# The order of the combined blocks in a two-layer trunk: T1, T2, T3, T4 for all features

## The chip, the cores and the metric

One core of a Trainium2 chip. The time is that of one execution on the device, in microseconds (us); the time of a kernel is the median of its runs.

## The reference

A trunk of two layers over 1024 positions of 1024 features. A mixer (gated delta rule in layer 0, retention in layer 1) and a feed-forward part with a causal convolution, each with a modulation before it and a layer norm behind it:

```python
D_MODEL = 1024; SEQ = 1024; DEPTH = 2; FFN_HIDDEN = 2816; FFN_CONV = 3
def conv_ffn(h, w_up, conv_w, conv_b, w_down):
    gate, up = jnp.split(h @ w_up, 2, axis=-1)
    gate = causal_dwconv(gate, conv_w) + conv_b
    return (jax.nn.silu(gate) * up) @ w_down
...
    for i in range(DEPTH):
        ...
        y = mixers[i % N_MIXERS](x * (1.0 + sc1) + sh1)
        x = layer_norm(DN_ALPHA * x + (1.0 + g1) * y, ln_g[i, 0], ln_b[i, 0])
        y = conv_ffn(x * (1.0 + sc2) + sh2, ffn_up[i], ffn_conv_w[i], ffn_conv_b[i], ffn_down[i])
        x = layer_norm(DN_ALPHA * x + (1.0 + g2) * y, ln_g[i, 1], ln_b[i, 1])
```

All of it is float32. The part that matters here is `h @ w_up` of both layers and retention's `h @ w_in`: a matrix of 1024 x 1024 activations times wide weights.

## The kernel before

Engines: PE does the matmuls, DVE (VectorE) tensor operations, ACT (ScalarE) activations and copies, SP issues most DMAs. Each engine works through its own queue in order; the order of each queue is set by the scheduler of the language's tile layer, which places instructions as their inputs are expected, so a change in the program text moves rows on every engine.

**A float32 matmul in three.** An operand is split into a rounded high part and the rest: ACT copies (`split`, L89), DVE subtracts (L90). `mm3` (L108 on) then does three matmuls, low x high, high x low and high x high, which appear as L110, L111 and L112 (or L1159, where a product is added to an accumulator that already holds one). A block of weights split in this way is called wb (512 wide) or wh and wl (1024 wide).

**Seven products in place of eight.** `strassen` multiplies 2 x 2 blocks of the activations (11, 12, 21, 22, by halves of features and of positions) with 2 x 2 blocks of the weights by the Strassen-Winograd scheme. It runs three times: for the input of the FFN of layer 0 (about 745 to 1190 us in the profile), for the input of retention (1425 to 1690) and for the FFN of layer 1 (2255 to 2700). The first two weight pairs are done plainly (`side`), while the activation blocks are still being made. From the third pair on, `wino` makes the seven products in this order: 11; 21; s1 with T1; s2 with T2 (added to the first); s4 with 22; s3 with T3; the last with T4. s1 to s4 are sums of weight blocks (`psub`, L1205), made by DVE into one of two `mm` PSUM banks and then split.

**The combined blocks.** T1 = 12 - 11, T3 = 22 - 12, T2 = T3 + 11, T4 = 21 - T2, each in four features k. `build_T` makes 12 and 22 (transposed on PE, scaled by ACT at L403 into a buffer bt, split), and returns `rest()`, which makes T1 to T4. `rest()` is called after the first weight pair's second half has been emitted. Blocks 11 and 21 exist only in split form; `joined` (L409) adds the two parts again by two matmuls with an identity into one of the two `mm` banks, which the transposes and the psubs use as well. Before, one join of 11 per feature served T2 and T1, and one join of 21 served T4. The rows of DVE are L423 (T3), L425 (T2), L427 (T1) and L429 (T4).

**Buffers.** `tags` names the pool of each block, in the order T1, T2, T3, T4, 22. A plain block 12 uses the pool of T1, so T1 can be split only when the last product on that block 12 is done.

Beside this, DVE does the convolution of the gate (L1584 three-operand rows, L1598 additions, L1570), the modulation of the next stage (L221, L223) and the weight splits. Line numbers above are those before; behind the change lines from L429 on stand one further down (L1205 is L1206, L1584 is L1585, L1159 is L1160).

Of the kernel before, what the change touches and what calls it, by code (L numbers as in the profile page):

```python
# [24 lines left out]
NF = F // P  # L25
# [8 lines left out]
def trunk_kernel(ctx: ExitStack, tc, A):  # L34
    nc = tc.nc
    pe, act, dve, pool, sp = nc.tensor, nc.scalar, nc.vector, nc.gpsimd, nc.sync
# [12 lines left out]
    def two(tag, dt=F32, name=None):  # L49
        if tag in ("qkv", "auh"):  # L50
            return tl(tag, [P, HALF], dt, name), tl(tag, [P, HALF], dt, name)
        t = tl(tag, [P, 2, HALF], dt, name)
        return t[:, 0], t[:, 1]
# [332 lines left out]

    def build_T(B, xts, scale, shift, tags):
        tags = dict(zip(("T1", "T2", "T3", "T4", "22"), tags))
        tags["12"] = tags["T1"]
        for nm in tags:  # L390
            B[nm] = [None] * 4

        def put(nm, k, src, eng=dve):
            t = two(tags[nm], F32R, nm)
            split(t[0], t[1], src, eng)
            B[nm][k] = t

        def load(f, tag):
            pt = mm_tile()
            for t in range(4):  # L400
                pe.transpose(pt[:, t * P:(t + 1) * P], xts[t][:, f * P:(f + 1) * P], ident)
            tmp = tl(tag, [P, HALF], name="bt")
            act.activation(tmp, pt, AF.Identity, bias=shift[:, f:f + 1], scale=scale[:, f:f + 1])  # L403
            return tmp

        def joined(hl):
            pt = mm_tile()
            for n, t in enumerate(hl):
                pe.matmul(pt, ident_r, t, start=n == 0, stop=n == 1)  # L409
            return pt  # L410

        raw = []
        for k, tg in enumerate((("qkv", "qkv"), ("qkv", "qkv"), ("t2", "t2"), ("t2", "ada"))):
            b12, b22 = load(k, tg[0]), load(4 + k, tg[1])
            put("12", k, b12)
            put("22", k, b22)
            raw.append((b12, b22))

        def rest():
            for k in range(4):  # L420
                t1, b22 = raw[k]
                x11 = joined(B["11"][k])
                dve.tensor_sub(b22, b22, t1)  # L423
                put("T3", k, b22)
                dve.tensor_add(b22, b22, x11)  # L425
                put("T2", k, b22)
                dve.tensor_sub(t1, t1, x11)  # L427
                put("T1", k, t1)
                dve.tensor_sub(b22, joined(B["21"][k]), b22)  # L429
                put("T4", k, b22)  # L430

        return rest
# [663 lines left out]
    for nm in ("S", "T0", "Dt", "M", "Tq"):  # L1096
# [4 lines left out]
    items = [("h", 1), ("h", 2), ("h", 3), (c, K + 3), (c, V), (c, V + 1), (c, 0), (c, 1), (c, V + 2), (c, V + 3), (c, 2), (c, 3),  # L1101
             (c, K + 4), (c, K + 5), (c, K + 6), (c, K + 7), (c, V + 4), (c, V + 5), (c, 4), (c, 5), (c, V + 6), (c, V + 7), (c, 6), (c, 7)]
# [47 lines left out]
        dve.tensor_tensor(b, a, b, ALU.add)  # L1150
        return b

    def strassen(hT0, xts, scale, shift, items, tags=("hTb", "hTb", "qkv", "qkv", "aux"), direct=False, beside=None, spare="lane"):
        B = {"11": hT0[:4], "21": hT0[4:]}
        nblk = [0]
        nacc = [0]

        def mm_on(*a, **kw):
            return pe.matmul(*a, skip_group_check=True, **kw)  # L1159

        def side(n, s):
            out = []
            for u in items[n][:2]:
                w = load_w(u)
                X = acc_tile()
                for i, b in enumerate((("11", "21"), ("12", "22"))[s]):
                    for k in range(4):
                        mm3(X, w, k + 4 * i, B[b][k], i == 0 and k == 0, i == 1 and k == 3)
                out.append(X)
            return out  # L1170

        ahead, sinks = [], []
        for n in range(2):
            X = side(n, 0)
            if direct:
                sinks.append(items[n][2]())
                for i in range(2):
                    sinks[n](2 * i, X[i], None)
                continue
            ahead.append([tl("cv", [P, 516], name="ah")[:, 0:HALF] for _ in range(2)])  # L1180
            for t, x in zip(ahead[n], X):
                act.activation(t, x, AF.Copy)
        rest = build_T(B, xts, scale, shift, tags)

        def block(src):
            n = nblk[0]
            nblk[0] += 1
            t = tl(("wh", "wl")[n % 2], [P, 2, HALF], F32R, name="wb")
            split(t[:, 0], t[:, 1], src)
            return kn(t[:, 0]), kn(t[:, 1])  # L1190

        def prod(src, b, onto=None):
            w = block(src)
            if onto is None:
                nacc[0] += 1
                acc = (acc_tile, acc_tile, sc_tile)[nacc[0] % 3]()
            else:
                acc = onto
            for k in range(4):
                mm3(acc, w, k, B[b][k], onto is None and k == 0, k == 3, mm_on if onto is not None else pe.matmul)  # L1200
            return acc

        def psub(x, y, op=ALU.subtract):
            t = mm_tile()
            dve.tensor_tensor(t, x, y, op)  # L1205
            return t  # L1206

        def wino(n, sink):
            ua, ub = items[n][:2]
            raws = []  # L1210
            for m, u in ((2 * n, ua), (2 * n + 1, ub)):
                if direct and m % 3 == 0:
                    raws += [tl("xT", [P, HALF], name="wr") for _ in range(2)]
                    for h2 in range(2):
                        anchor["i"] = sp.dma_start(raws[-2 + h2], u[:, hs(h2)])
                else:
                    w = tl("wr", [P, D])
                    anchor["i"] = sp.dma_start(w, u)
                    raws += [w[:, hs(0)], w[:, hs(1)]]
            if beside:  # L1220
                beside(n)
            a11, a12, a21, a22 = raws
            def copy_of(X, tag="cv"):
                t = tl(tag, [P, 516] if tag == "cv" else [P, HALF], name="pc")[:, 0:HALF]
                act.activation(t, X, AF.Copy)  # L1225
                return t

            X = prod(a11, "11")
            p1 = copy_of(X)
            s1 = psub(a21, a22, ALU.add)  # L1230
            sink(0, prod(a12, "21"), p1)
            s2 = psub(s1, a11)
            Z = prod(s1, "T1")
            z5 = copy_of(Z)
            s4 = psub(a12, s2)
            prod(s2, "T2", X)
            u2 = copy_of(X)
            s3 = psub(a11, a21)
            prod(s4, "22", Z)
            sink(1, Z, u2)  # L1240
            bg_step()
            prod(s3, "T3", X)
            u3 = copy_of(X, "t2")
            sink(3, X, z5)
            sink(2, prod(a22, "T4"), u3)
            bg_step()

        bg_tag[0] = spare
        for n in range(2):
            if not direct:  # L1250
                sinks.append(items[n][2]())
                for i in range(2):
                    sinks[n](2 * i, ahead[n][i], None)
            X = side(n, 1)
            for i in range(2):
                sinks[n](2 * i + 1, X[i], None)
            if n == 0:
                rest()
            if items[n][3]:
                items[n][3]()  # L1260
        for n in range(2, len(items)):
            wino(n, items[n][2]())
            if items[n][3]:
                items[n][3]()
        bg_tag[0] = "wr"
        return B
# [267 lines left out]
    def layer_tail(i, mix, wout, xsrc, x_mid, x_out, ln_next, final):  # L1534
        sc2, sh2 = fold(i, 1, 2 * i)
        if i == 0:
            hT0 = []
            get = out_hl(mix)
            G1 = rows[0, 2]
            xts = proj_ln(0, GH, get, wout, xsrc, G1, ("x", i))  # L1540
            hooks = ln_hooks(0, xts, "hTa", lambda: (sc2, sh2), hT0, x_mid, ("mid", i), BAL["gh"])
            xts = proj_ln(1, GH, get, wout, xsrc, G1, ("x", i), hooks=hooks, tag="aux")
# [3 lines left out]
        else:  # L1546
            mix.append((sc2, sh2))
            hT0, xts = proj_st(mix[0])
# [8 lines left out]
        spare = ("aux", "lane")[i]  # L1557
# [50 lines left out]

            return [(up[4 * fp], up[4 * fp + 2], gate_start, conv), (up[4 * fp + 1], up[4 * fp + 3], up_start, None)]

        strassen(hT0, xts, sc2, sh2, [it for fp in range(NF // 2) for it in pair_items(fp)], ("hTb", "hTb", "qkv", "qkv", ("lane", "aux")[i]), spare=spare)
        slots = {"c": "hTa", "x": "qkv"}
        gb2 = gain_rows(3, ("mid", i), "hTb") if final else None
        return proj_st(proj_gen(NF // 2, ablk_of(ad, "qkv"), A["ffn_down"][i], slots, xg[i + 1], rows[i, 5],
# [21 lines left out]
    h0, xts = layer_tail(0, raws, A["gdn_wout"], xin, xs[0], xs[1], next0, False)  # L1636
# [54 lines left out]
    sc_r, sh_r = next0()  # L1691
# [18 lines left out]
    order = units[:2]  # L1710
    for n in range(6):
        order += ropes[n + (n + 1) // 3:n + 1 + (n + 2) // 3] + [units[2 + n]]
    B = strassen(h0, xts, sc_r, sh_r, order, ("hTa", "aux", "qkv", "qkv", "hTa"), True, scale_rows)
    hT = [h0, []]
    xlo = []
    for t in range(4):
# [276 lines left out]
```

## Time and profile before

| | us |
|---|---|
| median of 3 runs | 2937.2 (2934.97, 2937.2, 2941.72) |
| profiled execution | 2931.49 |
| its span | 2929.3 |
| PE busy in it | 2808.1 |
| DVE busy in it | 2198.4 |
| granted TensorE clock, mean | 0.989 |

A row of a timeline has the start, the length, engine, line, operation and the tiles (written <- read); in brackets what the engine waited for just before it. A row of a window has the busy time and the number of instructions of PE, weight load, DVE, ACT and POOL, then the granted clock of PE (1.00 is full speed), the share of the DMA engines and GB/s. A matmul of a timeline row is shown with its whole length; the next one starts before it ends, so the starts count.

### The profile page before, as it was taken

How to read it: one execution, taken by the hardware profiler on the slowest of the kernel's cores; microseconds unless marked ns; L12 is line 12 of the kernel's file. 1: busy time of each engine (PE TensorE's matmuls, PEld its weight loads, DVE VectorE, ACT ScalarE, POOL GpSimd, SP SyncE). 2: the span in 40 equal slices, each digit the busy share in tenths (PEclk: the TensorE clock that was granted, in tenths of full speed). 3: DMA queues.
4: the chain of work that ended last, by engine and by line, in shares of the span. 5: the costliest groups of instructions: out<-in, count | busy, mean ns of one | idle time of the engine just before them, and what ended most of it. 6: DMA issues, size and time to landing. Idle time of an engine off the chain costs nothing. (4 is left out here: it accounts for less than half of the span.)

```text
span 2929.3 us, 38823 instructions
## 1 busy us (share of the span) xinstructions
PE 2808.1 (96%) x13638; PEld 2296.3 (78%) x13638; DVE 2198.4 (75%) x3965; ACT 1316.2 (45%) x2457; POOL 421.1 (14%) x485
## 2 busy tenths in 40 slices
PE   8998999999999999999999999999999899999997
PEld 7777877887778888887787877777778688888786
DVE  6695687556788888897687766666697887778888
ACT  3755465443544444536443332221345544444443
POOL 0311220134011111100000000223201011111001
PEclk9999999999999999999999999999999999999999
DMA  8122221354344444863434454555564233335753
GB/s 309 64 80 80 98 91 44 105 187 148 108 150 159 163 157 147 316 218 123 157 110 173 149 181 149 165 172 163 189 235 155 94 137 108 108 108 202 262 158 119
DMA packets 239234, 442.35 MB, mean 151 GB/s; under 512 B 22848, under 2 KB 76352, under 8 KB 239040
## 3 DMA queue, kind: packets, MB, share of 16 engines
q1 hardware_dynamic: 206832, 387.96, 39.4%
q10 hardware_dynamic: 29760, 43.00, 4.0%
q0 software_dynamic: 2448, 8.91, 0.8%
q8 instruction: 107, 1.75, 0.2%
q14 instruction: 87, 0.71, 0.1%
HBM read 331.26 MB, written 108.53 MB: 150 GB/s over the span
## 5 line engine op out<-in xcount | busy, mean ns | idle before, releaser
L1466 PE MATMUL acc<-bb,ab 128*128 128x512 f32 x1800 | 427.5, 393 | 6.5 <-DVE pa L1441 2.5
L1466 PEld LDWEIGHTS acc<-bb,ab 128*128 128x128 f32 x1800 | 338.0, 189 | 81.4 <-DVE bb L90 3.8
L630 PE MATMUL acc<-hT,wh 128*128 128x512 f32 x960 | 300.3, 394 | 0.0
L1605 POOL TENSOR_TENSOR o<-o 128x512 f32<-128x512 f32 x88 | 121.1, 1387 | 810.6 <-DVE o L1598 680.4
L89 ACT ACTIVATE ab<-ar 128x512 fp32r<-128x512 f32 x210 | 129.0, 624 | 184.2 <-PE acc L1466 93.3
L1159 PE MATMUL acc<-T,wb 128*128 128x512 f32 x840 | 204.2, 392 | 7.2 <-DVE wb L90 7.2
L630 PEld LDWEIGHTS acc<-hT,wh 128*128 128x128 f32 x960 | 183.0, 191 | 34.0
L630 PE MATMUL acc<-hT,wl 128*128 128x512 f32 x480 | 202.8, 422 | 0.8 <-DVE qkv L993 0.5
L1159 PEld LDWEIGHTS acc<-T,wb 128*128 128x128 f32 x840 | 157.9, 189 | 43.7 <-DVE wb L90 11.1
L90 DVE TENSOR_TENSOR ab<-ar,ab 128x512 fp32r<-128x512 f32 x210 | 146.4, 703 | 44.2 <-ACT ab L89 44.2
L90 DVE TENSOR_TENSOR wb<-mm,wb 128x512 fp32r<-128x512 f32 x216 | 145.2, 684 | 23.4 <-ACT wb L89 21.7
L90 DVE TENSOR_TENSOR wb<-wr,wb 128x512 fp32r<-128x512 f32 x162 | 111.3, 688 | 65.7 <-ACT wb L89 63.8
L1225 ACT ACTIVATE pc<-acc 128x512 f32<-128x512 f32 x143 | 84.7, 592 | 160.5 <-PE acc L1159 91.6
L89 ACT ACTIVATE wh<-wr 128x1024 fp32r<-128x1024 f32 x101 | 107.0, 1061 | 110.2 <-PE acc L630 50.3
L89 ACT ACTIVATE wb<-mm 128x512 fp32r<-128x512 f32 x216 | 122.3, 593 | 72.8 <-DVE mm L1205 72.1
L90 DVE TENSOR_TENSOR wl<-wr,wh 128x1024 fp32r<-128x1024 f32 x85 | 105.5, 1241 | 61.2 <-ACT wh L89 59.1
L89 ACT ACTIVATE wb<-wr 128x512 fp32r<-128x512 f32 x162 | 99.7, 627 | 96.5 <-DMA wr<-in_ffn_up 53.0
L449 DVE SCALAR_TENSOR_TENSOR qkv<-raw,vc,qkv 128x512 f32<-128x512 f32 x144 | 112.3, 783 | 34.8 <-ACT qkv L447 30.7
L630 PE MATMUL acc<-wh,hT 128*128 128x512 f32 x384 | 135.5, 415 | 0.7 <-DVE vv L90 0.7
L1584 DVE SCALAR_TENSOR_TENSOR o<-g,vc,o 128x512 f32<-128x512 f32 (+2 forms) x176 | 135.2, 786 | 0.7
L223 DVE SCALAR_TENSOR_TENSOR ada<-mvw,e,ada 128x512 f32<-128x512 f32 x140 | 105.9, 757 | 27.0 <-DMA mvw<-in_ada_w 26.5
L110 PE MATMUL acc<-T,wb 128*128 128x512 f32 x292 | 116.6, 399 | 9.9 <-DVE wb L90 9.4
(626 smaller groups left out, 6876.5 us busy)
## 6 DMA issues: line engine op xcount, KB each, us to landing
wr<-in_ffn_up SPq DMA_DIRECT2D x96, 512.0 KB, 4.3
ad<-o SPq DMA_DIRECT2D x154, 256.0 KB, 2.2
ar<-ad SPq DMA_DIRECT2D x154, 256.0 KB, 4.2
mvw<-in_ada_w SPq DMA_DIRECT2D x48, 512.0 KB, 5.5
Br<-in_ffn_down SPq DMA_DIRECT2D x66, 256.0 KB, 3.3
mvw<-in_ada_w SPq DMA_DIRECT2D x64, 256.0 KB, 3.0
wr<-in_ret_wv SPq DMA_DIRECT2D x32, 512.0 KB, 4.2
ar<-od SPq DMA_DIRECT2D x56, 256.0 KB, 5.0
```

The source lines that it names most:

```text
L89: act.activation(dst_h, src, AF.Copy)
L90: eng.tensor_tensor(dst_l, src, dst_h, ALU.subtract)
L110: mm(acc, wl[:, k], hl[0], start=first, stop=False)
L223: dve.scalar_tensor_tensor(a, wr[kk], e[:, k:k + 1], a, ALU.mult, ALU.add)
L449: dve.scalar_tensor_tensor(oh, raw[:, 3 - j:515 - j], w[:, 3 - j:4 - j], oh, ALU.mult, ALU.add)
L630: pq(pe.matmul(out, lhsT, rhs, start=start, stop=stop, **kw), cost)
L1159: return pe.matmul(*a, skip_group_check=True, **kw)
L1225: act.activation(t, X, AF.Copy)
L1466: mm_ = (lambda *a, p=p, onto=onto, **kw: (mm if p < 2 else pe.matmul)(*a, skip_group_check=onto, **kw))
L1584: dve.scalar_tensor_tensor(tv, gv[:, c0 - j:c1 - j], w[:, 2 - j:3 - j], tv, ALU.mult, ALU.add)
L1605: pool.tensor_tensor(o[d], o[x], o[y], op)
```

## The change

`rest()` makes T1 for all four features, then T2, then T3, then T4. T2 is now 22 - T1, without a join; T3 is T2 less a second join of 11, written into the buffer of T1's sum. The pools of T1 and T4 are exchanged in the FFNs (T1 now in `qkv`, T2 and T4 in `hTb`) and in retention (T1 in `qkv`, T4 in `hTa`), and block 12 shares the pool of T4.

```diff
-        tags["12"] = tags["T1"]
+        tags["12"] = tags["T4"]
...
         def rest():
-            for k in range(4):
-                t1, b22 = raw[k]
-                x11 = joined(B["11"][k])
+            for k, (t1, b22) in enumerate(raw):
+                dve.tensor_sub(t1, t1, joined(B["11"][k]))
+                put("T1", k, t1)
+            for k, (t1, b22) in enumerate(raw):
                 dve.tensor_sub(b22, b22, t1)
-                put("T3", k, b22)
-                dve.tensor_add(b22, b22, x11)
                 put("T2", k, b22)
-                dve.tensor_sub(t1, t1, x11)
-                put("T1", k, t1)
+            for k, (t1, b22) in enumerate(raw):
+                dve.tensor_sub(t1, b22, joined(B["11"][k]))
+                put("T3", k, t1)
+            for k, (t1, b22) in enumerate(raw):
                 dve.tensor_sub(b22, joined(B["21"][k]), b22)
                 put("T4", k, b22)
...
-    def strassen(hT0, xts, scale, shift, items, tags=("hTb", "hTb", "qkv", "qkv", "aux"), direct=False, beside=None, spare="lane"):
+    def strassen(hT0, xts, scale, shift, items, tags=("qkv", "hTb", "qkv", "hTb", "aux"), direct=False, beside=None, spare="lane"):
...
-        strassen(hT0, xts, sc2, sh2, [it for fp in range(NF // 2) for it in pair_items(fp)], ("hTb", "hTb", "qkv", "qkv", ("lane", "aux")[i]), spare=spare)
+        strassen(hT0, xts, sc2, sh2, [it for fp in range(NF // 2) for it in pair_items(fp)], ("qkv", "hTb", "qkv", "hTb", ("lane", "aux")[i]), spare=spare)
...
-    B = strassen(h0, xts, sc_r, sh_r, order, ("hTa", "aux", "qkv", "qkv", "hTa"), True, scale_rows)
+    B = strassen(h0, xts, sc_r, sh_r, order, ("qkv", "aux", "qkv", "hTa", "hTa"), True, scale_rows)
```

The number of operations stays the same on DVE and ACT; PE gets four more joins in each of the three stages. The queues differ as follows.

DVE in FFN 0 before, from the last T4 subtraction (the buffer bt_7129 is that of the last feature) to the split of s1 (mm_7422 holds s1, and wb_7443 is its split, for which T1's product waits). s1 itself was formed three rows above this piece:

```order
L429 TENSOR_TENSOR bt_7129<-mm_7293,bt_7129 128x512
L1205 TENSOR_TENSOR mm_7441<-mm_7422,wr_7400 128x512
L90 TENSOR_TENSOR T4_7298<-bt_7129,T4_7297 128x512
L1584 SCALAR_TENSOR_TENSOR o_7301<-g_7137,vc_153,o_7301 128x511
L1570 TENSOR_TENSOR g_7398<-sc_7427,pc_7420 128x512
L1584 SCALAR_TENSOR_TENSOR o_7306<-g_7137,vc_153,o_7306 128x512
L1584 SCALAR_TENSOR_TENSOR o_7301<-g_7137,vc_153,o_7301 128x510
L1584 SCALAR_TENSOR_TENSOR o_7311<-g_7138,vc_153,o_7311 128x511
L1584 SCALAR_TENSOR_TENSOR o_7316<-g_7138,vc_153,o_7316 128x512
L1584 SCALAR_TENSOR_TENSOR o_7306<-g_7137,vc_153,o_7306 128x512
L90 TENSOR_TENSOR wb_7443<-mm_7422,wb_7443 128x512
```

Behind the split of s1 stand, before, two more rows of this convolution and its four L1598 rows, two rows of the next convolution, two of the modulation and the third psub, and then the split of s2.

The same place after the change, from just behind the last T4 subtraction to the splits of s1 (mm_7434, wb_7455) and s2 (mm_7453, wb_7475):

```order
L1599 TENSOR_TENSOR o_7328<-o_7328,acc_7374 128x512
L1206 TENSOR_TENSOR mm_7434<-wr_7414 128x512
L90 TENSOR_TENSOR T4_7303<-bt_7109,T4_7303 128x512
L1585 SCALAR_TENSOR_TENSOR o_7554<-g_7410,vc_153,o_7554 128x511
L90 TENSOR_TENSOR T4_7310<-bt_7129,T4_7310 128x512
L1206 TENSOR_TENSOR mm_7453<-mm_7434,wr_7412 128x512
L1585 SCALAR_TENSOR_TENSOR o_7554<-g_7410,vc_153,o_7554 128x510
L221 TENSOR_SCALAR ada_7510<-mvw_7511,e_162 128x512
L90 TENSOR_TENSOR wb_7455<-mm_7434,wb_7455 128x512
L223 SCALAR_TENSOR_TENSOR ada_7510<-mvw_7511,e_162,ada_7510 128x512
L1206 TENSOR_TENSOR mm_7473<-wr_7412,mm_7453 128x512
L90 TENSOR_TENSOR wb_7475<-mm_7453,wb_7475 128x512
```

s1 is now formed behind all the T4 subtractions but ahead of two of their splits, and all eight L1585 rows and four L1599 rows of the earlier tile stand above the split of s1. Between the second feature's T1 subtraction and that split there are 51 rows.

PE in retention before, from the last products on block 11 (hT) to T1:

```order
L110 MATMUL sc_13233<-hT_12317,wb_13230 128x512
L111 MATMUL sc_13233<-hT_12317,wb_13230 128x512
L112 MATMUL sc_13233<-hT_12317,wb_13230 128x512
L110 MATMUL acc_13252<-T1_13055,wb_13249 128x512
L111 MATMUL acc_13252<-T1_13055,wb_13249 128x512
```

And after:

```order
L112 MATMUL sc_13257<-hT_12319,wb_13254 128x512
L409 MATMUL mm_13155<-hT_12329,ident_r_727 128x512 x2
L110 MATMUL sc_13257<-hT_12329,wb_13254 128x512
L111 MATMUL sc_13257<-hT_12329,wb_13254 128x512
L112 MATMUL sc_13257<-hT_12329,wb_13254 128x512
L110 MATMUL acc_13276<-T1_13058,wb_13273 128x512
L111 MATMUL acc_13276<-T1_13059,wb_13273 128x512
```

The last join of block 21 (mm_13155) has come to stand three matmuls ahead of T1's product; in FFN 0 it stands directly ahead of it.

DVE in retention after the change, behind that join:

```order
L430 TENSOR_TENSOR bt_12978<-mm_13155,bt_12978 128x512
L1151 TENSOR_TENSOR pc_13250<-sc_13257,pc_13250 128x512
L1206 TENSOR_TENSOR mm_13271<-mm_13252,wr_13230 128x512
L90 TENSOR_TENSOR T4_13159<-bt_12978,T4_13159 128x512
L90 TENSOR_TENSOR wb_13273<-mm_13252,wb_13273 128x512
```

The split of s1 (wb_13273), for which T1's product waits, stands four rows behind the last T4 subtraction. Before, it stood three rows behind it, and that subtraction's join stood 25 matmuls ahead of T1.

## The prediction

> **What bounds the kernel now.** I read the page's head first, then its costliest groups, then the list of PE's waits around the two feed-forward (FFN) stages where the combined blocks are made, and last the timelines of PE and DVE there.
>
> ```profile
> span 2929.3 us, 38823 instructions
> PE 2808.1 (96%) x13638; PEld 2296.3 (78%) x13638; DVE 2198.4 (75%) x3965; ACT 1316.2 (45%) x2457; POOL 421.1 (14%) x485
> ...
> L1159 PE MATMUL acc<-T,wb 128*128 128x512 f32 x840 | 204.2, 392 | 7.2 <-DVE wb L90 7.2
> ```
>
> PE is busy for 96% of the span, so only two things move the end: matmuls added or removed, and stretches in which PE stands or runs slowly. The last row is the products on combined blocks: they wait for DVE's split of a weight block (wb, L90). PE's waits in FFN 0 and, below the dots, FFN 1 (us in total, times, longest):
>
> ```profile
> PE acc L110 <- DVE wb L90: 4.7, 1, 4.7
> PE acc L1159 <- DVE wb L90: 1.9, 1, 1.9
> PE mm L409 <- DVE bt L429: 0.3, 1, 0.3
> ...
> PE acc L1159 <- DVE wb L90: 1.8, 1, 1.8
> PE sc L1159 <- DVE wb L90: 0.8, 1, 0.8
> ```
>
> FFN 1 has the 4.7 us too. PE's timeline says where (start, length; the wait in brackets): FFN 0, then FFN 1.
>
> ```profile
> 800.26 0.39 PE L112 MATMUL sc<-hT,wb 128*128 128x512 f32 x1
> 805.34 0.79 PE L110 MATMUL acc<-T,wb 128*128 128x512 f32 x1 [4.69 <-DVE wb L90]
> 805.93 0.63 PE L111 MATMUL acc<-T,wb 128*128 128x512 f32 x1
> 810.20 0.55 PE L112 MATMUL acc<-T,wb 128*128 128x512 f32 x1
> 812.64 4.41 PE L1159 MATMUL acc<-T,wb 128*128 128x512 f32 x12 [1.89 <-DVE wb L90]
> 819.84 0.39 PE L110 MATMUL acc<-T,wb 128*128 128x512 f32 x1
> ...
> 2313.50 0.79 PE L110 MATMUL acc<-T,wb 128*128 128x512 f32 x1 [4.69 <-DVE wb L90]
> 2323.64 0.84 PE L1159 MATMUL acc<-22_20065,wb 128*128 128x512 f32 x3
> 2326.36 0.39 PE L110 MATMUL acc<-T,wb 128*128 128x512 f32 x1
> ```
>
> The row at 805.34 is the first product on T1, 812.64 that on T2, then come the 12 matmuls on block 22, and 819.84 is the first on T4. FFN 1 is the same 1508.16 us later (2313.50 - 805.34), but its T4 starts at 2326.36, which is 818.20 on FFN 0's scale. At full speed a matmul is issued every (2326.36 - 2323.64)/12 = 0.227 us; T1 after its wait ran at (810.20 - 805.93)/10 = 0.427 us. The clock granted in these stretches (PEclk is the third number from the end):
>
> ```profile
> 805.30:810.75 5.45, 5.41 (x12) 3.79 (x12) 5.45 (x10) 2.55 (x5) 0.00 (x0) 0.52 0.13 50
> 815.00:817.00 2.00, 2.00 (x6) 1.52 (x6) 1.28 (x2) 0.60 (x1) 1.92 (x3) 0.50 0.14 25
> 2321.00:2325.00 4.00, 4.00 (x18) 3.28 (x18) 3.34 (x4) 1.09 (x2) 3.84 (x4) 1.00 0.44 150
> ```
>
> So the 4.69 us wait costs more than itself: T1's 12 matmuls took 5.41 us where 12 x 0.227 = 2.72 would do, a loss of 2.69. In FFN 0 the next 24 (812.64 to 819.84, 7.20 us against 5.44) lost 1.76 more. DVE's timeline shows why PE waited:
>
> ```profile
> 789.02 1.29 DVE L90 TENSOR_TENSOR wb<-wr,wb 128x512 fp32r<-128x512 f32 x2 [2.02 <-ACT wb L89]
> 796.16 1.29 DVE L90 TENSOR_TENSOR T<-bt,T 128x512 fp32r<-128x512 f32 x2
> 797.36 0.68 DVE L429 TENSOR_TENSOR bt<-mm,bt 128x512 f32<-128x512 f32 x1
> 801.29 3.39 DVE L1584 SCALAR_TENSOR_TENSOR o<-g,vc,o 128x512 f32<-128x512 f32 x5
> 804.60 0.69 DVE L90 TENSOR_TENSOR wb<-mm,wb 128x512 fp32r<-128x512 f32 x1
> 811.90 1.28 DVE L90 TENSOR_TENSOR wb<-mm,wb 128x512 fp32r<-128x512 f32 x2
> ```
>
> The split at 804.60 (s1) frees T1, the one at 811.90 (s2) frees T2. DVE is an in-order queue that works through without a gap there, and what counts is how many rows stand ahead of these two. Two rows of one tensor operation take (797.36 - 796.16) = 1.20, so 0.60 each; the convolution's rows (L1584) take 3.39/5, so 0.66 at their spacing.
>
> **The change, part by part.**
>
> *Operations.* DVE and ACT do the same number of them: per feature four subtractions and four splits stay. PE gets one more join of block 11 per feature, 4 in each of three stages (two FFNs and retention's input). What a join costs:
>
> ```profile
> 772.52 1.20 PE L409 MATMUL mm<-hT,ident_r 128*128 128x512 f32 x4 [0.58 <-ACT bt L403]
> ...
> 791.55 0.62 PE L409 MATMUL mm<-hT,ident_r 128*128 128x512 f32 x2
> 792.01 0.40 PE L111 MATMUL acc<-22_7074,wh 128*128 128x512 f32 x1
> ```
>
> 792.01 - 791.55 = 0.46, so 1.84 per stage and 5.5 in all. In the FFNs PE waits for DVE behind them, so the joins lie inside that wait and I charge nothing more; without that wait they would cost the full 3.7. In retention part of it is on the path, below.
>
> *FFN 0.* In the changed DVE queue the four T4 subtractions and splits, and the convolution's eight L1585 and four L1599 rows, all stand ahead of the split of s1. I walk the queue. T1 of the second feature needs its join, which before was one of the two at 772.52 and now stands behind 24 matmuls more (5.4 us, less the 1.0 of the wait and the join that no longer stand there): it runs from 776.95 to 777.4, and DVE starts that subtraction at about 777.65. From there to the end of the split of s1 stand 51 rows: 38 of 0.60, 2 splits of a 128x1024 block at 1.14, 10 three-operand rows at 0.66 and one of 0.4. That is 22.9 + 2.3 + 6.6 + 0.4 = 32.2, so 809.9, and T1 starts at 810.0 in place of 805.34. The PE queue is done with the products before it at about 801.8, so the wait grows from 4.69 to about 8.2. But the split of s2 now stands only three rows behind that of s1 and ends at 811.8 (811.9 to 812.5 before), while T1 is running, so the second wait is gone. The rest is then contiguous: 36 matmuls x 0.227 = 8.16 plus what the clock takes. The nearest row for that is the 4.69 wait with its 2.69, and I take it. T4 starts at 810.0 + 8.16 + 2.69 = 820.85, 1.0 later than 819.84. Bounds: with a clock loss of only 1.57 (below) and DVE 0.7 sooner, -0.8; with both losses of FFN 0 (2.69 + 1.76), +2.8.
>
> *FFN 1.* The orders of both engines are those of FFN 0. 820.85 against 818.20 is +2.65; bounds +0.8 and +4.4 in the same way.
>
> *Retention's input.* Here PE does not wait before T1 at all. PE's rows around it, a later wait of the same kind, and a shorter one in the next stage with their clocks:
>
> ```profile
> 1477.48 0.39 PE L112 MATMUL sc<-hT,wb 128*128 128x512 f32 x1
> 1477.71 0.48 PE L110 MATMUL acc<-T,wb 128*128 128x512 f32 x1
> ...
> 1561.78 4.45 PE L1159 MATMUL sc<-T,wb 128*128 128x512 f32 x12 [3.10 <-DVE wb L90]
> ...
> 1561.70:1563.70 2.00, 1.92 (x5) 1.54 (x6) 2.00 (x5) 0.00 (x0) 0.43 (x1) 0.50 0.75 285
> ...
> 2057.67 0.96 PE L630 MATMUL acc<-bb,ab 128*128 128x512 f32 x3 [2.75 <-DVE ab L90]
> ...
> 2057.00:2059.50 2.50, 1.83 (x7) 1.43 (x8) 2.11 (x5) 1.99 (x4) 0.00 (x0) 1.00 0.44 137
> ```
>
> Four joins now stand in a row ahead of the products on block 12 (about +0.34 left of it at the products on block 11), and two joins of block 21 stand among those products (0.92), the last only three matmuls from T1. PE comes to T1 at 1477.71 + 1.26 = 1479.0. That last join ends at 1478.3; behind it DVE has five rows in line up to the split of s1: T4's subtraction, an eviction (L1151), the psub of s2, T4's split, the split itself. With 0.25 to hand over, 5 x 0.60 and 0.2 back to PE, T1 starts at about 1481.8: a new wait of 2.8 and 4.1 later in all. The clock: a wait of 3.10 lost 1.57 (4.45 against 2.88 for its 12), one of 2.75 nothing; 2.8 lies at the second, so I take 0.4. Sum +4.5, ends +1.0 (the later 3.10 us wait takes it up, since DVE had been short of weights before it) and +5.7.
>
> *Buffers and queues.* T1 no longer waits for the last product on block 12; in both orders DVE reaches it after its join, so I cost it at nothing. T4 takes that wait over, and its product comes last; cover is the whole of T1, T2 and 22, 10 us. DMA issues on SP are as many as before; rows change places at the three transitions out of these stages, of which the FFNs' show no PE wait worth a microsecond at the seam, so nothing can be gained there, and I leave them at 0 with ends of -2 and +4 (the 4.69 us kind of wait, once).
>
> **Sum.** 1.0 + 2.65 + 4.5 = +8.2. The profiled execution took 2931.49, which makes 2939.7. The three runs' median is 2937.2 (2934.97 to 2941.72), 5.7 above it, so the forecast is 2945. What a measurement tells from no change is 0.2%, 5.9 us, so "slower" begins at 2943.1.
>
> [...]
>
> **The rivals.**
> - *The loss is taken up later, or the clock takes less.* Retention's DVE stood idle for weights after T1, so its delay may end in the 3.10 us wait: 1.0 + 2.65 + 1.0 = +4.7, 2942. Or the clock loses the 1.57 of the 3.10 us wait in the FFNs and nothing in retention: -0.1 + 1.5 + 4.1 = +5.5, 2943. For it speaks that 2.75 lost nothing; against it, that both 4.69 waits lost 2.69.
> - *Faster: T1 is ready early.* If DVE reaches the split of s1 before PE is at T1, both waits and their clock go: FFN 0 4.69 + 1.89 + 2.69 + 1.76, FFN 1 4.69 + 1.82 + 2.69, together 20.2, less 5.5 of joins: -14.7, 2922. For it: T1's own blocks are made first, and DVE had idle time (2.02 at 789.02) that earlier work may fill. Against it: T1's product waits for the split of s1 and not for T1, and that split now has the T4 rows ahead of it. With retention at +4.5 it decides "faster" if that split is done by about 803 in both FFNs, against my 809.9.
> - *Slower still: T4's buffers are held to the last product.* The down-projection's first blocks use the same buffers; a wait of the 4.69 us kind with its 2.69 at both seams gives 8.2 + 2 x 7.4 = +23, 2960. Against it: PE shows no wait there now.
> - *Nothing changes because the scheduler undoes it:* excluded, since the queues of DVE and PE differ.
>
> **How the numbers follow.** The forecast's mechanism 0.52, with its own range of 2940 to 2950; of that 0.08 lies below 2943.1. Taken up or smaller 0.27, faster 0.14, slower still 0.07. So slower 0.44 + 0.07 = 0.51, same 0.27 + 0.08 = 0.35, faster 0.14. The range leaves out the deep end of "faster" and the last rival: 2931 to 2955.
>
> **What would show it.** In the changed profile: T1's first matmul in FFN 0 near 810 with a wait of about 8 us on DVE's wb, no wait on T2, T4 near 820.9; in FFN 1 T4 near 2329.0; in retention a wait of about 2.8 us before T1 near 1481.8; 72 matmuls at the join's line where 48 were. Wrong it is if T1 starts before 805 in an FFN, if the second wait stays, or if the seams to the down-projections show a PE wait of several microseconds.

## The result, and the profile after

| us | before | after |
|---|---|---|
| median | 2937.2 (2934.13 to 2941.72, 5 runs) | 2953.24 (2948.33 to 2954.08, 5 runs) |
| profiled execution | 2931.49 | 2948.33 |
| its span | 2929.3 | 2946.6 |
| PE busy | 2808.1 | 2816.1 |

The changed kernel is slower: the ratio is 1.0047, 95% interval [1.0036, 1.0059], that is 14 us. The forecast was 2945 in a range of 2931 to 2955. The direction and the places were right; the loss is larger than the sum by a factor of about two.

PE's waits after, in FFN 0, in retention's input and in FFN 1 (us in total, times, longest):

```profile
PE acc L110 <- DVE wb L90: 11.2, 1, 11.2
PE mm L409 <- DVE bt L421: 1.0, 1, 1.0
...
PE acc L110 <- DVE wb L90: 2.8, 1, 2.8
...
PE acc L110 <- DVE wb L90: 11.2, 1, 11.2
```

The 4.7 before T1 in both FFNs has become 11.2, the second wait (L1159, now L1160) is gone from the FFNs, and retention has a wait before T1 that it did not have. PE's timeline, FFN 0, then retention, then FFN 1, each from T1's first matmul (FFN 0's and FFN 1's last row is the first matmul on T4):

```profile
813.73 0.79 PE L110 MATMUL acc<-T,wb 128*128 128x512 f32 x1 [11.17 <-DVE wb L90]
818.10 2.91 PE L1160 MATMUL acc<-T,wb 128*128 128x512 f32 x12
823.57 0.39 PE L110 MATMUL acc<-T,wb 128*128 128x512 f32 x1
...
1486.81 0.80 PE L110 MATMUL acc<-T,wb 128*128 128x512 f32 x1 [2.80 <-DVE wb L90]
1492.10 3.26 PE L1160 MATMUL acc<-T,wb 128*128 128x512 f32 x12
...
2334.48 0.80 PE L110 MATMUL acc<-T,wb 128*128 128x512 f32 x1 [11.17 <-DVE wb L90]
2345.05 0.39 PE L110 MATMUL acc<-T,wb 128*128 128x512 f32 x1
```

One profile differs from the next by several microseconds ahead of these stages already, so I compare each stage within itself: from the first matmul on block 12 to the first on T4, from PE's timelines of each kernel.

| first matmul on 12 to first on T4, us | FFN 0 | retention | FFN 1 | the three against before |
|---|---|---|---|---|
| before | 55.97 | 43.57 | 54.35 | |
| after | 59.31 | 50.38 | 60.06 | +15.9 |
| forecast of the difference | +1.0 | +4.5 | +2.65 | +8.2 |
| measured difference | +3.3 | +6.8 | +5.7 | +15.9 |

The spans differ by 17.3. 15.9 of it lies in these three places; the rest is spread over the stretches before, between and behind them, 1.4 at most in one, either way.

DVE's timeline of FFN 0 after shows what the walk of the queue had missed:

```profile
778.00 1.29 DVE L421 TENSOR_TENSOR bt<-bt,mm 128x512 f32<-128x512 f32 x2 [2.62 <-PE mm L409]
...
806.58 1.75 DVE L1585 SCALAR_TENSOR_TENSOR o<-g,vc,o 128x511 f32<-128x511 f32 x1
808.25 1.75 DVE L90 TENSOR_TENSOR T<-bt,T 128x512 fp32r<-128x512 f32 x1
809.92 0.69 DVE L1206 TENSOR_TENSOR mm<-mm,wr 128x512 f32<-128x512 f32 x1
810.52 1.15 DVE L1585 SCALAR_TENSOR_TENSOR o<-g,vc,o 128x510 f32<-128x510 f32 x1
811.59 1.49 DVE L221 TENSOR_SCALAR ada<-mvw,e 128x512 f32<-128x512 f32 x1
813.00 0.68 DVE L90 TENSOR_TENSOR wb<-mm,wb 128x512 fp32r<-128x512 f32 x1
```

The walk put the T1 subtraction behind its join at 777.65 (it came at 778.00) and the end of the split of s1 at 809.9. The order and the count of rows were right; up to 806.58 the queue kept to the walk. Then four rows took 1.67, 1.67, 1.07 and 1.41 by their spacing, where 0.66, 0.60, 0.66 and 0.39 had been put: 3.5 us. The one row among them that reads a PSUM bank (L1206) was as short as ever. POOL's timeline has the partner:

```profile
805.54 7.25 POOL L1606 TENSOR_TENSOR o<-o 128x512 f32<-128x512 f32 x4 [54.66 <-DVE o L1599]
```

These are POOL's four sums of gated blocks, which start when the last L1599 row is done. The change brought those rows ahead of the split of s1, and POOL's sums with them.

FFN 0 from its first matmul on block 12 to the end of the split of s1, before and then after (DVE's busy time and rows are the third pair):

```profile
763.87:805.29 41.42, 34.69 (x155) 26.49 (x153) 34.85 (x53) 27.82 (x47) 0.00 (x0) 0.98 0.15 51
764.26:813.68 49.42, 36.16 (x163) 28.24 (x161) 43.44 (x63) 30.06 (x50) 7.10 (x4) 0.93 0.21 75
```

DVE worked 8.6 us longer there and stood idle no longer (6.6 before, 6.0 after). So the 8.0 us by which T1 came later in this stage are ten more rows ahead of the split and the 3.5 us; the 2.62 us wait for a join at 778.00 took the place of other waits. Retention is different: up to T1, DVE worked 1.1 us longer and stood idle 2.9 longer (8.5 against 5.6), and its waits for joins grew from 0.8 to 3.7.

### The profile page after: what moved, and what is told of

It reads as the page before. It is cut to its first block, busy times and chain, and to the rows that moved or that the text cites. A ratio compares the mean times of both kernels' runs of the same rounds, so it can differ in the third digit from the quotient of the medians.

```text
span 2946.6 us, 38847 instructions
## 1 busy us (share of the span) xinstructions
PE 2816.1 (96%) x13662; PEld 2306.4 (78%) x13662; DVE 2202.3 (75%) x3965; ACT 1318.2 (45%) x2457; POOL 420.4 (14%) x485
## 5 line engine op out<-in xcount | busy, mean ns | idle before, releaser
L1160 PE MATMUL acc<-T,wb 128*128 128x512 f32 x840 | 203.2, 391 | 3.8 <-DVE wb L90 3.8
L1160 PEld LDWEIGHTS acc<-T,wb 128*128 128x128 f32 x840 | 157.6, 188 | 39.2 <-DVE wb L90 6.5
L1585 DVE SCALAR_TENSOR_TENSOR o<-g,vc,o 128x512 f32<-128x512 f32 (+2 forms) x176 | 138.1, 802 | 0.9 <-ACT o L1580 0.2
```

Of the source, the lines that this page charges most:

```text
L1585: dve.scalar_tensor_tensor(tv, gv[:, c0 - j:c1 - j], w[:, 2 - j:3 - j], tv, ALU.mult, ALU.add)
```

## The experiments

**POOL beside DVE.** The changed kernel, in which POOL makes the four sums of each FFN's first gated tile on one column in place of 512 and leaves out the rest of them. All queues keep their order.

```diff
-                            pool.tensor_tensor(o[d], o[x], o[y], op)
+                            pool.tensor_tensor(*[t[:, :HALF if fp else 1] for t in (o[d], o[x], o[y])], op)
```

> The changed kernel, with POOL's four sums of the first gated tile of each FFN done on one column in place of 512 (those sums are left out of the rest of the tile); every queue keeps its order. Theory POOL: four DVE rows ahead of the split of s1 took 1.67, 1.67, 1.07 and 1.41 us in place of 0.66, 0.60, 0.66 and 0.39 because POOL's sums ran beside them, 3.5 us in all; T1's first matmul in FFN 0 comes back from 813.73 to about 810.2, and both FFNs together give 7 us: 2953.2 becomes about 2946. Rival DMA: the rows were stretched by the transfers that ran in that stretch (0.39 of the DMA engines), then T1 stays near 813.7 and the time near 2953.

2944.49 us (2940.39 to 2952.09), ratio to before 1.0027 [1.0014, 1.0040]: 8.7 less than the changed kernel by the medians, about 6 by the two ratios. The same DVE rows in FFN 0:

```profile
812.66 0.74 DVE L1585 SCALAR_TENSOR_TENSOR o<-g,vc,o 128x511 f32<-128x511 f32 x1
813.32 0.68 DVE L90 TENSOR_TENSOR T<-bt,T 128x512 fp32r<-128x512 f32 x1
```

And PE's waits before T1 in FFN 0 and FFN 1:

```profile
PE acc L110 <- DVE wb L90: 7.6, 1, 7.6
...
PE acc L110 <- DVE wb L90: 7.7, 1, 7.7
```

The rows are back at 0.66 and 0.60, and the wait at 7.6 and 7.7 where the prediction had 8.2. The theory holds for the rows and the waits: 3.5 us of the wait in each FFN were POOL's. It was not the transfers, the rival: the DMA engines' share beside these rows was 0.67 here (809.5 to 816) and 0.39 in the changed kernel (806.5 to 813). The three stages took 58.65, 47.58 and 56.14 against 59.31, 50.38 and 60.06, so FFN 1 gained 3.9, but FFN 0 only 0.7. In this profile FFN 0 lost clock that the changed kernel's profile did not lose: 1.6 us at its joins (granted 0.79 over 8 us, against 1.00), and 11.2 us from T1 to T4 in place of 9.8.

**The clock behind a short wait.** The changed kernel with 11 filler matmuls in retention's wait, and the changed kernel profiled once more.

```diff
...
+            if direct and b == "T1" and not warm:
+                warm.append(1)
+                for _ in range(11):
+                    pe.matmul(acc, ident_r, B["11"][0][0], start=True, stop=True)
```

> The changed kernel with 11 further matmuls of block 11 with the identity written into T1's accumulator in retention before the product starts it anew (2.5 us of work into a wait of 2.80). Theory clock: what follows the 2.80 us wait lost about 2.8 us because the clock was at half; with the wait filled T1's 12 matmuls take 2.72 and not 5.4, T1 starts where it did (within 0.3), and the time falls by 2 to 3: about 2950.5. Rival: the loss behind T1 comes from the weights that DVE splits late (T2's and 22's), then the time stays near 2953 and a wait appears in their place.

> The changed kernel once more, for a second profile. Theory: the clock behind a wait of 2.8 us in retention falls in some executions and not in others; from T1 to T4 there takes either 11.1 us (half clock) or 8.3 (full clock), with the same 2.80 before T1. Rival: the half clock follows from this kernel's own order of work, then 11.1 again.

With the filler retention's stage took 47.61 us in place of 50.38, T1 started where it did, and nothing was lost behind it. But the median did not move: 2953.01 (2944.86 to 2955.71), ratio 1.0049 [1.0036, 1.0062]. The second profile of the changed kernel (one execution, 2951.81 us) offers a reason. (In the filler's own profile FFN 0's stage also took 62.05 in place of 59.31.) That second profile has the same 2.80 us wait and no half clock behind it, and its retention stage took 47.63. The four microseconds from T1's start, in the changed kernel's first profile (PEclk is the third number from the end):

```profile
1486.80:1490.80 4.00, 3.99 (x9) 3.15 (x10) 2.61 (x5) 1.69 (x3) 0.00 (x0) 0.50 0.00 0
```

and in its second, with T1's row from the timeline below:

```profile
1491.10:1495.10 4.00, 3.93 (x17) 3.23 (x18) 2.61 (x5) 1.69 (x4) 0.00 (x0) 1.00 0.00 0
```

```profile
1491.17 0.50 PE L110 MATMUL acc<-T,wb 128*128 128x512 f32 x1 [2.80 <-DVE wb L90]
```

So a 2.80 us wait is followed by half clock in some executions and not in others (in one of three profiles; the third is that of the POOL experiment, with the same wait and a stage of 47.58). The lateness in retention is 4.1 us, as forecast; whether the 2.8 of clock behind it come on top depends on the execution. Why it comes and goes behind the same wait, no run here shows.

**The pools and the order apart.** New order and second join with the old pools, and the old order with the new pools. The edit of the first against the changed kernel (the two calls of `strassen` get their old pools in the same way):

```diff
-        tags["12"] = tags["T4"]
+        tags["12"] = tags["T1"]
...
-tags=("qkv", "hTb", "qkv", "hTb", "aux")
+tags=("hTb", "hTb", "qkv", "qkv", "aux")
```

> The order T1, T2, T3, T4 and the second join, with the pools as they were before (T1 and T2 in hTb, T3 and T4 in qkv, block 12 with T1). Theory pools: in the FFNs it is the exchange of pools that lets the convolution's rows come ahead of the split of s1; here that split stands behind 45 rows and seven convolution rows, T1 starts near 806.5 and T4 near 821 in FFN 0 (+1 against before, FFN 1 +2), retention keeps its +7: about 2947. Rival order: the order of the T blocks itself makes the FFNs late, then 2953 as in the changed kernel.

> The order and the joins as before, with the new pools alone (T1 and T3 in qkv, T2 and T4 in hTb, block 12 with T4). Theory pools: eight convolution rows and four additions stand ahead of the split of s1 again, POOL's sums start early and stretch DVE's rows, T1 in FFN 0 comes near 811 to 813 and both FFNs lose 2 to 4 each; retention is as before: about 2943. Rival order: 2937, T1 near 805 as before.

The first was a miss: 2956.52 us (2955.06 to 2961.12), ratio 1.0069 [1.0057, 1.0081], no better than the changed kernel; its stages took 58.34, 53.41 and 59.92. The second: 2941.25 (2934.87 to 2943.41), ratio 1.0011 [1.0002, 1.0019], that is 0.6 to 5.6 us; its stages took 56.03, 43.63 and 55.78, so in these three places the pools alone cost about 1.5. They do let the convolution come first (the wait before T1 in FFN 0 is 9.0), but the second wait goes in exchange, so the stages did not lose the 2 to 4 each that were expected. The DVE waits of the first, in FFN 0:

```profile
DVE bt L430 <- PE mm L409: 3.4, 2, 3.2
DVE bt L421 <- PE mm L409: 3.2, 1, 3.2
```

DVE, the engine on which everything hangs here, stood for 6.6 us waiting for joins, against 0.2 in this stage of the kernel before. That pointed to the joins, which the prediction had priced as PE time, but for the one wait in its walk.

**The second join alone.** The kernel before, with one line changed:

```diff
-                dve.tensor_sub(t1, t1, x11)
+                dve.tensor_sub(t1, t1, joined(B["11"][k]))
```

> The kernel before, old order and old pools, in which T1 takes a second join of block 11 of its own: the part of the change that adds joins, alone. Theory joins hidden in the FFNs: 24 matmuls more, of which 1.8 us show in retention and up to 1 in each FFN: about 2940. Rival: the joins go through the two mm banks that s1 needs too, DVE falls behind, T1 in retention gets a wait of 2 to 3 as in the changed kernel: 2944 and more.

2953.11 us (2951.34 to 2955.50), ratio 1.0047 [1.0033, 1.0062]: a loss as large as that of the whole change, from 24 matmuls of which each pair takes 0.46 us of PE. Its stages took 58.10, 52.39 and 58.09, that is +2.1, +8.8 and +3.7. The sum, 14.7, is close to the change's 15.9, but it is spread otherwise (+3.3, +6.8 and +5.7 there). DVE in retention, at the subtractions that follow a join:

```profile
1462.02 0.69 DVE L429 TENSOR_TENSOR bt<-mm,bt 128x512 f32<-128x512 f32 x1 [4.31 <-PE mm L409]
1469.51 0.69 DVE L429 TENSOR_TENSOR bt<-mm,bt 128x512 f32<-128x512 f32 x1 [0.56 <-PE mm L409]
1480.53 0.69 DVE L429 TENSOR_TENSOR bt<-mm,bt 128x512 f32<-128x512 f32 x1 [3.18 <-PE mm L409]
```

A join stands in PE's queue behind the matmuls that were placed ahead of it; DVE's queue stops at the subtraction until PE gets there (8.0 us in three waits here), and what stands behind it is late, the split of s1 too: T1 starts 7.5 us later in this stage. DVE's waits for joins up to T1, in the three stages, are 2.9, 8.0 and 2.9 us in this kernel, 0.2, 0.8 and 0.2 in the kernel before, and 2.6, 3.7 and 2.7 in the changed one (waits of 0.2 us and more).

**Grouping with one join.** The changed kernel's pools and grouping, but T3 made first, so that T1 and T2 share a join again (the lines that make the blocks, as they are then; the T4 loop stays):

```diff
...
+            for k, (t1, b22) in enumerate(raw):
+                dve.tensor_sub(b22, b22, t1)
+                put("T3", k, b22)
+            for k, (t1, b22) in enumerate(raw):
+                x11 = joined(B["11"][k])
+                dve.tensor_sub(t1, t1, x11)
+                put("T1", k, t1)
+                dve.tensor_add(b22, b22, x11)
+                put("T2", k, b22)
...
```

> The changed kernel's pools, with blocks grouped over all features as in the change, but T3 = 22 - 12 made first, then T1 and T2 from one shared join of 11, then T4: 24 matmuls fewer than the changed kernel. Theory join: the second join is what costs 14 us, grouping and pools little; about 2941. Rival order: grouping over all features puts all T4 rows ahead of the split of s1 and costs as much as the joins; 2948 and more.

2929.54 us (2925.62 to 2934.34), ratio 0.9970 [0.9959, 0.9981]: not 2941, but 8 us faster than before. Its stages took 48.30, 46.90 and 48.37: the FFNs gained 7.7 and 6.0, retention lost 3.3. In FFN 0 no DVE row waits 0.2 us or more for a join any more, and PE takes up T1 after a wait of 0.1. The splits of s1 and s2:

```profile
806.89 0.69 DVE L90 TENSOR_TENSOR wb<-mm,wb 128x512 fp32r<-128x512 f32 x1
812.02 0.68 DVE L90 TENSOR_TENSOR wb<-mm,wb 128x512 fp32r<-128x512 f32 x1
```

This stage began 4.51 later than before's (768.38 against 763.87), so the split of s1 ends at 803.1 on before's scale. The prediction's rival "faster" named 803 as the point from which it decides. This experiment changes two things against the changed kernel, the join and the place of T3; how the gain divides between them was not tried apart.

Side by side, the kernels with one join of block 11 took 2937 (before), 2941 (new pools) and 2930 us (this one), and those with two 2953 (the change), 2957 (old pools) and 2953 (old order, old pools). So the loss goes with the second join: added alone it costs as much, and no order or pools tried with it avoided the loss. How it comes to cost that much is shown by DVE's waits in the old order and in retention. In the changed kernel's FFNs, where DVE did not wait longer, the loss lies in the rows ahead of the split and in POOL; what part of these rows is due to the join and what to the order was not tried apart.

**The half clock under T1.** The kernel before with 19 filler matmuls in each FFN's 4.69 us wait, in the same way as above.

> The kernel before with 19 further matmuls of block 11 with the identity in each FFN, written into T1's accumulator before the product starts it anew: 4.3 us of work into the wait of 4.69. Theory clock: T1's 12 matmuls take 2.72 and not 5.41; from T1 to T4 12.0 in place of 14.5 in FFN 0 and 10.2 in place of 12.9 in FFN 1, though the second wait can grow by as much as T1 ends sooner: the split of s2 still ends at 812.5, so FFN 0 keeps its T2 at 812.64 and gains only the clock behind it, 1.8, and FFN 1 nothing: 2935. Rival: without the half clock both FFNs gain 2.7: 2931.5.

2941.39 us (2938.03 to 2944.15), ratio 1.0007 [0.9999, 1.0016]. T1 ran at full clock (its matmuls 0.23 us apart, 0.427 before), and the next product waited for what T1 no longer took:

```profile
811.22 0.50 PE L110 MATMUL acc<-T,wb 128*128 128x512 f32 x1 [0.25 <-DVE wb L90]
818.51 4.61 PE L1160 MATMUL acc<-T,wb 128*128 128x512 f32 x12 [4.29 <-DVE wb L90]
```

FFN 0's stage stayed at 55.98: from T1 to T2 it took 7.29 us (7.30 before), and from T2 to T4 7.21 (7.20 before). FFN 1's rose from 54.35 to 56.81. Before, it took 5.56 from T2 to T4, with 0.98 granted over T2; if T2 now ran there at the half clock as in FFN 0, with 7.21 to T4, that is 1.65 of the 2.46, an estimate. So in FFN 0 of the kernel before, T1's 2.69 us of clock loss lay wholly beside DVE's way to the split of s2. With a later wait on the same engine behind it, that loss was no term of the sum.

**The weight split first.** The kernel before, with s1, s2 and their splits given a higher priority in the scheduler for the first pair. In the first of two runs the splits of s1 and s2 are also written ahead of the product on 21 in every pair, so that PE's order changes there too (T1 came ahead of 21 in the first pair). In the second the FFNs do this for the first pair only, and retention for all. The edit of the second:

```diff
...
+            if n == 2 or direct:
+                with (tc.high_priority(offset=300) if n == 2 else nullcontext()):
+                    s1 = psub(a21, a22, ALU.add)
+                    w1 = block(s1)
+                    s2 = psub(s1, a11)
+                    w2 = block(s2)
+                sink(0, prod(a12, "21"), p1)
+                Z = prod(w1, "T1")
...
```

> The kernel before (old order, old pools), in which the sums s1 and s2 of the first seven-product pair and their splits are given a higher priority in the scheduler, so that in the FFNs the split of s1 stands two rows behind T1's last split and PE's queue reads 11, T1, 21, T2, 22. Theory of the late weight split: T1 starts near 798.8 on FFN 0's scale in place of 805.34, with waits of about 1 before T1 and T2 and 2 before 22; T4 near 813, that is 7 less in FFN 0 and 5 less in FFN 1, retention the same: about 2925. Rival: the rows of DVE are only exchanged, 21 and T2 wait for what T1 no longer waits for, and the time stays at 2937.

> The kernel before, with the early splits of s1 and s2 for the first seven-product pair of each FFN only, and, in retention, the order s1, s2 ahead of 21 for all pairs, as in the earlier experiment, whose FFN stages took 5.4 and 5.3 us less up to T4 and 8.6 and 12.5 more behind it. Theory: what was lost behind T4 came from the order of the products in the later pairs (T1 ahead of 21); with that order undone in the FFNs the stage gain stays: FFN 0 and FFN 1 each about 5 less, retention 6.8 less, 2922. Rival: the first pair's early splits themselves push DVE's later rows back, then the FFNs give the gain back behind T4 and the time is 2930 to 2937.

The first gave 2936.93 (2931.64 to 2943.59), ratio 0.9996 [0.9986, 1.0006]: a miss. Up to T4 the FFN stages were 5.4 and 5.3 shorter (50.58 and 49.02), but from T4 to the start of their last product 8.2 and 10.9 longer (383.32 against 375.17, 378.25 against 367.34; the 8.6 and 12.5 above were read from a row inside that product), and retention's was 6.8 shorter from its first matmul on block 12 to there (298.87 against 305.69). The second keeps the one and drops most of the other: 2920.23 us (2914.75 to 2922.91), ratio 0.9935 [0.9918, 0.9953], the fastest of all kernels here. Its FFN stages took 48.99 each, and from T4 to the last product 376.95 and 371.19, 1.8 and 3.9 longer than before; retention again took 298.8 in all. DVE in FFN 0, and below it PE at T1:

```profile
797.39 1.29 DVE L90 TENSOR_TENSOR T<-bt,T 128x512 fp32r<-128x512 f32 x2
798.59 0.69 DVE L429 TENSOR_TENSOR bt<-mm,bt 128x512 f32<-128x512 f32 x1
799.19 0.68 DVE L90 TENSOR_TENSOR wb<-mm,wb 128x512 fp32r<-128x512 f32 x1
```

```profile
799.93 0.50 PE L110 MATMUL acc<-T,wb 128*128 128x512 f32 x1 [0.79 <-DVE wb L90]
```

The split of s1 stands two rows behind T1's last split, and the wait of 4.69 is one of 0.79. In retention PE waited 7.8 us for DVE's split weight blocks (wb) before; now its list of waits holds only these two:

```profile
PE sc L1159 <- ACT pc L1225: 3.1, 4, 0.8
PE acc L110 <- DVE wl L90: 1.3, 1, 1.3
```

## Why the prediction was right or wrong

- **Direction and place: right.** T1 became late for the split of s1 behind it, not for T1 itself; the second wait went, retention got a wait of 2.80 (2.8 forecast) and the join's line has 72 matmuls.
- **FFN 0, +1.0; measured +3.3.** The mis-sized term is "51 rows, 32.2 us". It measured 3.5 more, since the durations were those of rows with POOL at rest. POOL is not in the walk at all: that the change triggers its sums earlier, beside the rows on the path, is what the step left out. The trace of before held the price: there too a row ran beside POOL's sums, behind the split of s2, where no wait of PE followed from it:

```profile
812.06 5.91 POOL L1605 TENSOR_TENSOR o<-o 128x512 f32<-128x512 f32 x4 [61.57 <-DVE o L1598]
813.82 1.78 DVE L1205 TENSOR_TENSOR mm<-wr 128x512 f32<-128x512 f32 x1
```

  The clock went the other way: 2.69 was put behind T1, and T1 with T2 and 22 lost 9.84 - 8.16 = 1.7.
- **FFN 1, +2.65; measured +5.7.** The same 3.5, with a clock loss of 10.57 - 8.16 = 2.4 for 2.69.
- **Retention, +4.5; measured +6.8, and 4.1 in the second profile.** The lateness of 4.1 was right. The clock term (0.4 between two rows, 2.75 without and 3.10 with a loss) was 2.8 in one execution and 0 in another, behind the same 2.80 us wait, so the length of the wait alone could not decide it.
- **The sum.** +8.2, and 7.0 for POOL in both FFNs, 2.4 for the clock in retention, less 1.3 for the clock in the FFNs, makes 16.3; the three places measured 15.9. The median, 2953.24, is above the 2940 to 2950 that the prediction gave its own mechanism. It lies in the full range of 2931 to 2955, near its end, which owes something to luck: the two terms that were too small, POOL and the clock in retention, were not what the range was widened for.
- **Two yardsticks for the clock.** The prediction set T1's 5.41 us in the FFNs against 2.72 for 12 matmuls, and the 4.45 in retention against 2.88. By the second, which like the 5.41 runs to the end of the last matmul, the 2.69 is 2.5.
- **"In the FFNs the joins lie inside the wait, and I charge nothing more": not what the sum missed, but wrong as a price.** The walk had the one long wait for a join in it (777.65; measured 778.00), and the FFNs' miss is POOL and clock. But in the kernel with the second join alone, to which the same pricing gave about 2940, the FFNs lost 2.1 and 3.7 and retention 8.8. The price of a join there is DVE's wait for it and not PE's time.
- **The rival "taken up later":** did not happen. From T4 to the start of its last product retention took 262.09 after and 262.12 before. Its other half, that the clock takes less, came true in retention in two of three profiles.
- **The rival "faster":** its mechanism exists, but it needs the joins out of DVE's way or the split of s1 ahead of the T4 rows. Three kernels have such an early split in FFN 0, at 803.1 and near 799 on before's scale. Two are faster; the third, the first with the weight split early, gained 5.4 and 5.3 us up to T4 and gave them back behind it.
- **T4's buffers and the seams:** nothing to see, as costed. From T4 to the start of the last product the FFNs took 374.74 and 366.30 (before 375.17 and 367.34), and in the 30 us from there on PE shows no wait at either seam.

## What to carry to other kernels

Where two in-order queues feed each other, price an added operation by what its reader's queue waits until it is reached, not by its own duration alone: twelve joins of 0.46 us of PE each, added alone, cost 14 us here. Walk the queue that the waiting engine depends on row by row, and ask for each stretch which other engine now runs beside it (POOL's sums beside four DVE rows cost 3.5 us in each FFN here). Look for the row on which the wait ends (the split of s1), and move that forward; T1's blocks, made first by this change, started no product sooner.

## What the runs showed of the hardware

- DVE rows whose tensor inputs all lie in SBUF slowed down while POOL ran its four sums of 128x512 (7.25 us). In the changed kernel's FFN 0 a 128x511 three-operand row went from 0.66 to 1.67 us, one of 128x510 to 1.07, a split from 0.60 to 1.67 and a one-operand row (L221) from 0.39 to 1.41, while a row that reads PSUM stayed at 0.60. With the sums on one column the 128x511 row and the split took 0.66 and 0.60 again. Not every such row paid: in the kernel grouped with one join, one three-operand row beside POOL's sums took 0.67 and the next 1.09. Why rows slow down, and why not all of them, no run here shows.
- PE's clock fell behind waits as short as 2.80 us in one execution and not in the next (granted 0.50 and 1.00 over the 4 us from T1's start), and in the POOL experiment even behind the 1.0 and 0.4 us waits at FFN 0's joins (granted 0.79 over 8 us, where the changed kernel's own profile has 1.00), which is 1.6 us of that stage; the profile of the filler in retention has the same 0.79 there. A single profile does not settle a term of that size.
